# Row factor of the RMS norms: two narrow fp32 products rewritten as pairs of fp32r products over high and low halves

## The chip, the cores and the metric

The kernel runs on one core of one Trainium2 chip. The metric is the device time of one execution in microseconds. TensorE (PE in the profile, with its weight loads PEld) multiplies, VectorE (DVE), ScalarE (ACT) and GpSimd (POOL) work elementwise, and SyncE (SP) issues DMAs. Each engine runs its own instructions in a fixed order and waits on semaphores for the others.

## The reference, cut to what matters

The program is a trunk of two layers over 512 tokens of width 1024. Each layer has a SwiGLU feed-forward half step, a mixer (layer 0 a bidirectional state-space scan, layer 1 a two-dimensional neighbourhood attention), a second feed-forward half step, and a gated embedding. Every one of these starts with an RMS norm:

```python
def rmsnorm(x, g):
    xf = x.astype(jnp.float32)
    y = xf * lax.rsqrt(jnp.mean(xf * xf, axis=-1, keepdims=True) + RMS_EPS)
    return (y * g.astype(jnp.float32)).astype(x.dtype)

for i in range(DEPTH):
    h = h + 0.5 * swiglu(rmsnorm(h, ffn1_norm[i]), ffn1_w_gu[i], ffn1_w_down[i])
    hn = rmsnorm(h, mix_norm[i])
    h = h + mixer(hn)          # the state-space mixer norms its own output once more
    h = h + 0.5 * swiglu(rmsnorm(h, ffn2_norm[i]), ffn2_w_gu[i], ffn2_w_down[i])
    gate = jax.nn.sigmoid(rmsnorm(h, ple_norm[i]) @ ple_w_gate[i])
    h = h + gate * rmsnorm(p[i] @ ple_w_proj[i], ple_post_norm[i])
```

That makes eleven row factors of 512 tokens each: five per layer, and one inside the state-space mixer.

## The kernel before, in words

Activations lie transposed: 128 channels on the partitions, 512 tokens along the free dimension, eight such tiles `h[0..7]`. All large products are made of fp32r operands (fp32 rounded to fewer bits): each fp32 tensor is split into a high part, a cast to fp32r, and a low part, the rest. A product is then three matmuls, high by high, high by low and low by high, on lines 278, 281 and 282 (512 columns) or 508, 509 and 510 (256 columns, the feed-forward blocks that save a multiplication). Weights arrive by DMA as fp32 (`wr`, `md`), ACT casts the high part (L221, `wh`) and DVE subtracts the low part (L223, `wl`), up to three units ahead of TensorE.

The gain of a norm is folded into the split of `h`, and the matmuls start before the row factor is known; the factor is multiplied in when a result leaves PSUM. The factor itself is made in two steps. While the last channels of `h` are produced, ACT squares each tile (L328) and DVE or POOL adds the squares into one tile `acc` (L332). Then `begin` sums over the partitions: four fp32 matmuls, each with 128 tokens of `acc` as the stationary operand and one column of 1/1024 as the moving one (L346), which leave the means of 512 tokens as a 128x4 tile. DVE scales them (L349) and takes the reciprocal square root in two integer and nine floating operations on 128x4 elements (`newton_rsqrt`, L313 to L319, result `self.y`). Some matmuls later `end` spreads the factors again: four fp32 matmuls whose stationary operand is one column of `y`, broadcast to 128 columns, and whose moving operand is the identity (L356); ACT copies the 128x512 result to SBUF (L359), and only then can results that wait for it leave PSUM. An fp32 matmul of the program stands in the trace as two weight loads and two matmuls.

`begin` is called at eleven places. In this text they are numbered by time: 0 first feed-forward of layer 0, 1 state-space mixer, 2 the norm inside it, 3 second feed-forward, 4 norm of the embedding (`ple_proj`), 5 gate of the embedding; 6 to 10 the same for layer 1, without the inner norm: 6 feed-forward, 7 attention, 8 feed-forward, 9 embedding, 10 gate. A scheduler sets the order of each engine's instructions from the order in which they are written, their dependences and its own estimate of their lengths; at run time the order is fixed, and an instruction that waits holds up everything behind it on its engine. The tag `sq` has four buffers of 128x512.

Of the kernel before, what the change touches and what calls it, by code (L numbers as in the profile page):

```python
# [8 lines left out]
F32R = mybir.dt.float32r  # L9
I32 = mybir.dt.int32  # L10
AF = mybir.ActivationFunctionType
ALU = mybir.AluOpType
AX = mybir.AxisListType

P = 128
# [10 lines left out]
EPS = 1e-6  # L26
NH = 32
NG = 8
NC = T // P
# [41 lines left out]
def trunk(ctx, tc, A, out):  # L71
    nc = tc.nc
    v, s, g, te, sy = nc.vector, nc.scalar, nc.gpsimd, nc.tensor, nc.sync


    cp = ctx.enter_context(tc.tile_pool(name="cp", bufs=1))
# [10 lines left out]
    def nm(t):  # L87
        uid[0] += 1
        return f"{t}{uid[0]}"

    def sm(shape, dt=F32):
        return sp.tile([P] + list(shape), dt, name=nm("sm"), tag="sm", bufs=12)

    def slot(tag, bufs):
        return lambda dt=F32: bp.tile([P, T], dt, name=nm(tag), tag=tag, bufs=bufs)

    hs, t2, sc, sq = slot("hs", 8), slot("t2", 7), slot("sc", 15), slot("sq", 4)

    def md(dt=F32):
        return bp.tile([P, 2, T], dt, name=nm("md"), tag="md", bufs=24)  # L100
# [4 lines left out]
    def rt():  # L105
        return bp.tile([P, T], F32, name=nm("rt"), tag="rt", bufs=3)

    def bank(tag, bufs):
        return ps.tile([P, T], F32, name=nm("ps"), tag=tag, bufs=bufs)

    mm_bank = lambda: bank("mm", 5)
    px_bank = lambda: bank("px", 3)
# [5 lines left out]
    ones_d = cp.tile([P, P], F32, name="ones_d")  # L118
# [4 lines left out]
        te.matmul(out=idle[:, :P], lhsT=ones_d, rhs=ones_d, start=True, stop=True)  # L123
    warm = cp.tile([P, 1], F32, name="warm")
    ident = msk[:, M_ID:M_ID + P]

    def col(i):
        return cst[:, i:i + 1]
# [13 lines left out]
    stop = A.get("stage", 4 * DEPTH)  # L142
# [86 lines left out]
    def prep_next():  # L229
        item = next(todo, None)  # L230
        if item is None:
            return False
        what, a = item
        if what == "u":
            split_raw(*take())
        elif what == "g":
            group[:] = [take()[0] for _ in range(4)]
        elif what == "s":
            p, i = a
            a21, a11, a22, a12 = group  # L240
            if i == 0:
                blocks[p] = {0: a11, 2: a21, 3: wide(), 4: a12, 6: a22}
                v.tensor_add(out=blocks[p][3], in0=a21, in1=a22)
            elif i == 1:
                blocks[p][1] = blocks[p][5] = wide()
                v.tensor_sub(out=blocks[p][1], in0=blocks[p][3], in1=a11)
            else:
                v.tensor_sub(out=a21, in0=a11, in1=a21)
        else:
            p, i = a  # L250
            b = blocks[p]
            split_raw(b[i], 1024)
            if i == 1:
                v.tensor_sub(out=b[5], in0=b[4], in1=b[5])
        top_up()
        return True
# [16 lines left out]
    def gemm(pt, w, pairs, first=True, last=True, off=0, cols=slice(0, T), behind=False):  # L273
        hi, lo = w
        n = len(pairs)
        for k, xp in enumerate(pairs):
            sl = slice((off + k) * P, (off + k + 1) * P)
            m = te.matmul(out=pt, lhsT=hi[:, sl], rhs=part(xp, 0, cols), start=first and k == 0, stop=False)  # L278
            if behind and k == 0:
                tc.keep_in_program_order(m)  # L280
            te.matmul(out=pt, lhsT=hi[:, sl], rhs=part(xp, 1, cols), start=False, stop=False)  # L281
            gemm.last = te.matmul(out=pt, lhsT=lo[:, sl], rhs=part(xp, 0, cols), start=False,  # L282
                                  stop=last and k == n - 1)
# [27 lines left out]
    def newton_rsqrt(m, y, a):  # L311

        v.tensor_scalar(out=y.bitcast(I32), in0=m.bitcast(I32), scalar1=1, scalar2=None, op0=ALU.arith_shift_right)  # L313
        v.tensor_scalar(out=y.bitcast(I32), in0=y.bitcast(I32), scalar1=-1, scalar2=0x5F3759DF,
                        op0=ALU.mult, op1=ALU.add)
        for _ in range(3):
            v.tensor_mul(out=a, in0=y, in1=y)
            v.scalar_tensor_tensor(out=a, in0=a, scalar=-0.5, in1=m, op0=ALU.mult, op1=ALU.mult)
            last = v.scalar_tensor_tensor(out=y, in0=a, scalar=1.5, in1=y, op0=ALU.add, op1=ALU.mult)  # L319
        return last  # L320

    class SumSq:
# [8 lines left out]
            else:  # L331
                (v if fast else g).tensor_add(out=self.acc, in0=self.acc, in1=q)  # L332

        def rsqrt(self, scale=1.0, eps=EPS):
            pt = px_bank()
            te.matmul(out=pt, lhsT=ones_d, rhs=self.acc, start=True, stop=True)
            m, a, y = sc(), sc(), rt()
            v.tensor_scalar(out=m, in0=pt, scalar1=scale, scalar2=eps, op0=ALU.mult, op1=ALU.add)
            newton_rsqrt(m, y, a)
            return y  # L340

        def begin(self, scale=1.0, eps=EPS):

            pt = px_bank()
            for c in range(NC):
                te.matmul(out=pt[:, c:c + 1], lhsT=self.acc[:, c * P:(c + 1) * P], rhs=ones_d[:, :1],  # L346
                          start=True, stop=True)
            m, a, self.y = sm([NC]), sm([NC]), sm([NC])
            v.tensor_scalar(out=m, in0=pt[:, :NC], scalar1=scale, scalar2=eps, op0=ALU.mult, op1=ALU.add)  # L349
            self.last = newton_rsqrt(m, self.y, a)  # L350

        def end(self):

            pt = px_bank()
            for c in range(NC):
                te.matmul(out=pt[:, c * P:(c + 1) * P], lhsT=self.y[:, c:c + 1].to_broadcast([P, P]), rhs=ident,  # L356
                          start=True, stop=True)
            r = rt()
            s.copy(out=r, in_=pt)  # L359
            return r  # L360

    class Norm:
# [14 lines left out]

        def count(self, k, fast=False):
            self.ss.add(h[k], fast=fast or k == KD - 1)

        def factor(self):
            return self.ss.rsqrt()

        def begin(self, half=False):
            if half:
# [8 lines left out]
    def ffn(norm, nxt, between=None, first=None, at=4):  # L394
# [9 lines left out]
        def gate_up(f):  # L404
# [3 lines left out]
            if first and f < 2:  # L408
                held.append((f, pg, pu))
                if f == 1:  # L410
                    first([p for x in held for p in x[1:]], norm.pairs)
                    mid()
                return
# [1016 lines left out]
    def first(pts, pairs):  # L1430
        done_ = [0] * 4
        here, cut_ = 0, [0] * 4
        for o in order:
            if isinstance(o, int):
                here = o + 1
            else:
                cut_[o[0]] += 1
            for u in range(4):
                while done_[u] < min(here, 4 * cut_[u]):
                    k = done_[u]  # L1440
                    gemm(pts[u], begun[u][2:], pairs[k:k + 1], first=k == 0, last=k == KD - 1, off=k)
                    done_[u] += 1
        prep_next()

        with tc.issue_after(splits[-1].ins):
            for k in range(KD):
                n.count(k, True)
        while len(ready) < 3:
            prep_next()

    for i in range(stop):
        l, w = divmod(i, 4)
        last = i == stop - 1
        m = None if last else Norm(gains[i + 1], (lambda: md(F32R)) if w == 2 else xa)
# [112 lines left out]
```

## Time and profile before

| what | value |
|---|---|
| median of 3 runs | 2305.32 us (2305.17 to 2305.44) |
| the profiled execution's own time | 2305.77 us |
| its span, first to last instruction | 2304.0 us |
| PE busy | 2292.0 us, 99% |
| DVE busy | 1826.6 us, 79% |
| ACT busy | 1179.0 us, 51% |
| L346 (begin): loads and matmuls on PE | 88 and 88 |
| L356 (end): loads and matmuls on PE | 88 and 88 |

Times in the profile's timeline are microseconds from the start of the span: a row gives start, length, engine, line, operation, output and inputs, shape and count, and in brackets the engine's idle time before it with what ended it. Matmuls are pipelined, so the length of one (0.39 us) is longer than the step from one to the next (0.23 us); it is the steps that add up. A row of PEld is a weight load, which runs beside the matmul before it.

### The profile page before, as it was taken

To read this page: it belongs to the slowest core of one execution; us is meant where nothing else is said; L and a number is where in the kernel's file an instruction comes from. 1 tells how busy PE (TensorE), PEld (TensorE's weight loads), DVE (VectorE), ACT (ScalarE), POOL (GpSimd) and SP (SyncE) were. 2 spreads that over 40 slices of the span, in tenths; PEclk is the share of its full clock that TensorE was granted. 3 is DMA by queue.
4 is the path that set the end of the run, shared out by engine and by line. 5 is a ranking of instruction groups with operands and counts; after the bars stand their busy time and mean duration, and the time that the engine had idled before them with its cause. 6 is when DMAs were issued, how large, how long until landed. Compare 5 with 4: busy or idle time off the path is not lost.

```text
span 2304.0 us, 35426 instructions
## 1 busy us (share of the span) xinstructions
PE 2292.0 (99%) x13732; PEld 2025.5 (88%) x13732; DVE 1826.6 (79%) x2621; ACT 1179.0 (51%) x2038; POOL 323.7 (14%) x261
## 2 busy tenths in 40 slices
PE   9999999999999999999999999999999999999999
PEld 8899998888888888999998889999878888999987
DVE  7878878888788958987885897787578859887866
ACT  5433445877676864444445444444446745444452
POOL 0000001355555641000003100000110010000020
PEclk9999999999999999999999999999999999999999
DMA  5323323444444543333223233232557732333222
GB/s 185 116 83 106 110 73 130 164 155 138 146 140 151 188 158 119 106 101 106 94 78 104 101 102 107 84 102 83 165 183 220 219 119 83 111 106 101 87 92 73
DMA packets 105224, 281.69 MB, mean 122 GB/s; under 512 B 13136, under 2 KB 14032, under 8 KB 105056
## 3 DMA queue, kind: packets, MB, share of 16 engines
q1 hardware_dynamic: 104768, 279.30, 37.0%
q8 instruction: 107, 1.75, 0.3%
q14 instruction: 61, 0.50, 0.1%
q10 hardware_dynamic: 288, 0.14, 0.0%
HBM read 259.70 MB, written 13.40 MB: 119 GB/s over the span
## 4 chain that ended last, share of the span: by engine, by line
PE 95%; DVE 3%; DMA 1%; ACT 1%; issue 0%; SPq 0%; POOL 0%; ACTq 0%; POOLq 0%
PE ps L278 19%; PE ps L282 19%; PE ps L281 19%; PE ps L510 10%; PE ps L509 10%; PE ps L508 10%; PE ps L930 1%; PE ps L889 1%; PE ps L910 1%; PE ps L1325 1%; PE ps L1271 1%; DVE wl L223 1%; PE ps L845 1%; PE ps L834 1%; DVE md L304 1%; PE ps L1314 0%
## 5 line engine op out<-in xcount | busy, mean ns | idle before, releaser
L278 PE MATMUL ps<-md,wh 128*128 128x512 f32 (+1 forms) x2032 | 798.6, 393 | 0.0
L282 PE MATMUL ps<-md,wl 128*128 128x512 f32 (+1 forms) x2032 | 790.5, 389 | 1.6 <-DVE wl L223 1.6
L281 PE MATMUL ps<-md,wh 128*128 128x512 f32 (+1 forms) x2032 | 791.2, 389 | 0.0
L221 ACT CAST wh<-wr 128x1024 fp32r<-128x1024 f32 (+2 forms) x395 | 351.8, 892 | 500.9 <-PE ps L281 260.1
L223 DVE TENSOR_TENSOR wl<-wr,wh 128x1024 fp32r<-128x1024 f32 (+2 forms) x395 | 418.5, 1061 | 84.4 <-ACT wh L221 82.6
L282 PEld LDWEIGHTS ps<-md,wl 128*128 128x128 f32 x2032 | 381.5, 188 | 83.5 <-DVE wl L223 2.9
L278 PEld LDWEIGHTS ps<-md,wh 128*128 128x128 f32 x2032 | 382.2, 188 | 73.8 <-issue 0.7
L281 PEld LDWEIGHTS ps<-md,wh 128*128 128x128 f32 x2032 | 382.4, 188 | 71.5
L221 ACT CAST wh<-md 128x1024 fp32r<-128x1024 f32 x175 | 183.6, 1049 | 322.6 <-PE ps L509 296.1
L332 POOL TENSOR_TENSOR sq<-sq,sq 128x512 f32<-128x512 f32 x71 | 101.0, 1422 | 1637.7 <-ACT sq L328 1633.3
L510 PE MATMUL ps<-sc,wl 128*128 128x256 f32 x980 | 277.5, 283 | 0.8 <-DVE wl L223 0.8
L508 PE MATMUL ps<-sc,wh 128*128 128x256 f32 x980 | 276.9, 283 | 0.8 <-ACT wh L221 0.8
L509 PE MATMUL ps<-md,wh 128*128 128x256 f32 x980 | 277.4, 283 | 0.1
L510 PE MATMUL ps<-md,wl 128*128 128x256 f32 x980 | 277.3, 283 | 0.0
L509 PE MATMUL ps<-sc,wh 128*128 128x256 f32 x980 | 277.3, 283 | 0.0
L508 PE MATMUL ps<-md,wh 128*128 128x256 f32 x980 | 277.2, 283 | 0.0
L514 DVE TENSOR_TENSOR t<-ps,t 128x512 f32<-128x512 f32 x245 | 165.8, 689 | 137.6 <-PE ps L510 137.0
L223 DVE TENSOR_TENSOR wl<-md,wh 128x1024 fp32r<-128x1024 f32 x175 | 213.4, 1219 | 16.3 <-ACT wh L221 15.9
L508 PEld LDWEIGHTS ps<-sc,wh 128*128 128x128 f32 x980 | 187.7, 192 | 4.9 <-ACT wh L221 1.0
L509 PEld LDWEIGHTS ps<-sc,wh 128*128 128x128 f32 x980 | 187.7, 192 | 3.9
L509 PEld LDWEIGHTS ps<-md,wh 128*128 128x128 f32 x980 | 188.0, 192 | 1.6 <-DVE md L472 0.4
L508 PEld LDWEIGHTS ps<-md,wh 128*128 128x128 f32 x980 | 188.0, 192 | 1.3
(209 smaller groups left out, 2895.5 us busy)
## 6 DMA issues: line engine op xcount, KB each, us to landing
wr<-in_w_gw_dram SPq DMA_DIRECT2D x70, 512.0 KB, 3.5
md<-in_w_gw_dram SPq DMA_DIRECT2D x70, 512.0 KB, 5.0
wr<-in_w_in_dram SPq DMA_DIRECT2D x65, 512.0 KB, 3.5
wr<-in_w_dn_dram SPq DMA_DIRECT2D x128, 256.0 KB, 2.6
wr<-in_w_gu_dram SPq DMA_DIRECT2D x32, 512.0 KB, 3.5
hs<-crow SPq DMA_DIRECT2D x64, 256.0 KB, 3.7
wr<-in_w_dn_dram SPq DMA_DIRECT2D x32, 384.0 KB, 3.0
wr<-in_w_qkv_dram SPq DMA_DIRECT2D x24, 512.0 KB, 4.3
```

Source lines behind the costliest of these rows:

```text
L221: splits.append(s.copy(out=hi[:, :n], in_=raw[:, :n]))
L223: v.tensor_sub(out=lo[:, :n], in0=raw[:, :n], in1=hi[:, :n])
L278: m = te.matmul(out=pt, lhsT=hi[:, sl], rhs=part(xp, 0, cols), start=first and k == 0, stop=False)
L281: te.matmul(out=pt, lhsT=hi[:, sl], rhs=part(xp, 1, cols), start=False, stop=False)
L282: gemm.last = te.matmul(out=pt, lhsT=lo[:, sl], rhs=part(xp, 0, cols), start=False, stop=last and k == n - 1)
L304: split.low = v.tensor_sub(out=dst[:, 1, :], in0=src, in1=dst[:, 0, :])
L332: (v if fast else g).tensor_add(out=self.acc, in0=self.acc, in1=q)
L508: te.matmul(out=o, lhsT=hi[:, sl], rhs=xh, start=j == 0 and kk == 0, stop=False)
L509: te.matmul(out=o, lhsT=hi[:, sl], rhs=xl, start=False, stop=False)
L510: te.matmul(out=o, lhsT=lo[:, sl], rhs=xh, start=False, stop=j == 1 and kk == 3)
L514: v.tensor_add(out=k[to], in0=pt, in1=k[other])
L834: te.transpose(out=pt[:, cs(i)], in_=src[:, cs(c)], identity=ident)
```

## The change

`begin` first splits `acc`: ACT casts it to a high half in fp32r, DVE subtracts for the low half, both 128x512, in two more buffers of the tag `sq`. Its four fp32 matmuls become eight fp32r ones, two for each 128 tokens (high and low half as stationary operand, added up in PSUM), with two equal columns of 1/1024 (`mean`) as the moving operand. The mean and the reciprocal root are now 128x8 instead of 128x4. After the root, DVE splits `y` into two halves (a cast and a subtraction, 128x8). `end` becomes eight fp32r matmuls, high and low half of each column broadcast, by an fp32r copy of the identity (`identr`). `mean` and `identr` are made once, on ACT, `mean` at the very start and `identr` in the first feed-forward behind the squares. An unused function of 128x512 factors goes.

```diff
@@ -123,6 +123,9 @@
     ident = msk[:, M_ID:M_ID + P]
+    mean = cp.tile([P, 2], F32R, name="mean")
+    s.copy(out=mean, in_=ones_d[:, :2])
+    identr = cp.tile([P, P], F32R, name="identr")
@@ -331,30 +334,31 @@
         def begin(self, scale=1.0, eps=EPS):
 
+            hi, lo = sq(F32R), sq(F32R)
+            s.copy(out=hi, in_=self.acc)
+            v.tensor_sub(out=lo, in0=self.acc, in1=hi)
             pt = px_bank()
             for c in range(NC):
-                te.matmul(out=pt[:, c:c + 1], lhsT=self.acc[:, c * P:(c + 1) * P], rhs=ones_d[:, :1],
-                          start=True, stop=True)
-            m, a, self.y = sm([NC]), sm([NC]), sm([NC])
-            v.tensor_scalar(out=m, in0=pt[:, :NC], scalar1=scale, scalar2=eps, op0=ALU.mult, op1=ALU.add)
-            self.last = newton_rsqrt(m, self.y, a)
+                for x, part_ in enumerate((hi, lo)):
+                    te.matmul(out=pt[:, 2 * c:2 * c + 2], lhsT=part_[:, c * P:(c + 1) * P], rhs=mean,
+                              start=x == 0, stop=x == 1)
+            m, a, y = sm([2 * NC]), sm([2 * NC]), sm([2 * NC])
+            v.tensor_scalar(out=m, in0=pt[:, :2 * NC], scalar1=scale, scalar2=eps, op0=ALU.mult, op1=ALU.add)
+            newton_rsqrt(m, y, a)
+            self.y = sm([2, 2 * NC], F32R)
+            v.tensor_copy(out=self.y[:, 0], in_=y)
+            self.last = v.tensor_sub(out=self.y[:, 1], in0=y, in1=self.y[:, 0])
 
         def end(self):
 
             pt = px_bank()
             for c in range(NC):
-                te.matmul(out=pt[:, c * P:(c + 1) * P], lhsT=self.y[:, c:c + 1].to_broadcast([P, P]), rhs=ident,
-                          start=True, stop=True)
+                for x in range(2):
+                    te.matmul(out=pt[:, c * P:(c + 1) * P],
+                              lhsT=self.y[:, x, 2 * c:2 * c + 1].to_broadcast([P, P]), rhs=identr,
+                              start=x == 0, stop=x == 1)
             r = rt()
             s.copy(out=r, in_=pt)
             return r
@@ -1445,6 +1446,7 @@
         with tc.issue_after(splits[-1].ins):
             for k in range(KD):
                 n.count(k, True)
+        s.copy(out=identr, in_=ident)
```

Line numbers behind the change are three higher in this part of the file (L221 becomes L224, L223 L226, L328 L331, L332 L335), and the new lines are L340 (cast of `acc`), L341 (its low half), L345 (matmuls of `begin`), L348 (scale), L351 and L352 (split of `y`) and L359 (matmuls of `end`).

The change moves instructions. First place: ACT and DVE at norm 6, the first feed-forward of layer 1. ACT before:

```order
L306 ACTIVATE md_12767<-hs_8795,cst 128x512
L328 ACTIVATE sq_12770<-hs_8795 128x512
L221 CAST wh_12791<-wr_12693 128x1024
L221 CAST wh_12876<-wr_12795 128x1024
L359 COPY rt_12899<-ps_12894 128x512
```

ACT now:

```order
L309 ACTIVATE md_12861<-hs_8844,cst 128x512
L331 ACTIVATE sq_12864<-hs_8844 128x512
L340 CAST sq_12939<-sq_12596 128x512
L224 CAST wh_12885<-wr_12787 128x1024
L224 CAST wh_12981<-wr_12889 128x1024
L363 COPY rt_13008<-ps_12999 128x512
```

The cast of `acc` stands ahead of two weight casts. DVE at the end of the same norm's root, before (L319 is the last operation of the root, L243 the first of the next feed-forward's weight sums):

```order
L317 TENSOR_TENSOR sm_12851<-sm_12852 128x4
L318 SCALAR_TENSOR_TENSOR sm_12851<-sm_12851,sm_12850 128x4
L319 SCALAR_TENSOR_TENSOR sm_12852<-sm_12851,sm_12852 128x4
L243 TENSOR_TENSOR md_12869<-wr_12779,md_12787 128x1024
L246 TENSOR_TENSOR md_12871<-md_12869,wr_12785 128x1024
```

DVE now:

```order
L320 TENSOR_TENSOR sm_12953<-sm_12954 128x8
L321 SCALAR_TENSOR_TENSOR sm_12953<-sm_12953,sm_12952 128x8
L322 SCALAR_TENSOR_TENSOR sm_12954<-sm_12953,sm_12954 128x8
L351 CAST sm_12967<-sm_12954 128x8
L352 TENSOR_TENSOR sm_12967<-sm_12954,sm_12967 128x8
L246 TENSOR_TENSOR md_12974<-wr_12873,md_12881 128x1024
```

Two operations more stand between the root and everything behind it on DVE. Second place: ACT in the first feed-forward of the program, behind norm 0, where casts of activations (L441 and L303 are a SiLU and a split, L471 and L492 splits of sums) stand among casts of weights (L221). Before:

```order
L441 ACTIVATE t_463<-t_463 128x512
L471 CAST sc_411<-t_472 128x256
L303 CAST md_469<-t_466 128x512
L221 CAST wh_527<-wr_350 128x1024
L303 CAST md_478<-t_474 128x512
L492 CAST sc_481<-t_485 128x512
```

Now:

```order
L442 ACTIVATE t_482<-t_482 128x512
L224 CAST wh_546<-wr_365 128x1024
L306 CAST md_488<-t_485 128x512
L472 CAST sc_430<-t_491 128x256
L306 CAST md_497<-t_493 128x512
L493 CAST sc_500<-t_504 128x512
```

The weight cast has moved ahead of the two casts L303 and L471. Third place: PE at norm 4, the embedding's, whose `begin` stands among the products of a feed-forward's last chunk. Before, it stood between two groups of eighteen matmuls:

```order
L281 MATMUL ps_12185<-md_11960,wh_12123 128x512
L282 MATMUL ps_12185<-md_11959,wl_12125 128x512
L346 MATMUL ps_12217<-ones_d,sq_12034 128x1 x4
L278 MATMUL ps_12237<-md_11367,wh_12154 128x512
L281 MATMUL ps_12237<-md_11368,wh_12154 128x512
```

Now:

```order
L285 MATMUL ps_12312<-md_11731,wl_12220 128x512
L345 MATMUL ps_12285<-mean,sq_12281 128x2
L281 MATMUL ps_12312<-md_12023,wh_12218 128x512
L284 MATMUL ps_12312<-md_12024,wh_12218 128x512
L285 MATMUL ps_12312<-md_12023,wl_12220 128x512
L345 MATMUL ps_12285<-mean,sq_12282 128x2
L345 MATMUL ps_12285<-mean,sq_12281 128x2
```

It has moved twelve matmuls later, and its first matmul, on the high half, stands three matmuls ahead of the second, on the low half. Norm 9 moves in the same way. At the other nine norms `begin` stands at the same place on PE, and `end` at the same place or, at norms 1, 6 and 7, one matmul later.

More of the change, by code (lines that the diff above doesn't have):

```diff
@@ L332, in add @@
                 (v if fast else g).tensor_add(out=self.acc, in0=self.acc, in1=q)
[L334 to L340, printed above, removed]
         def begin(self, scale=1.0, eps=EPS):
+            hi, lo = sq(F32R), sq(F32R)
+            s.copy(out=hi, in_=self.acc)
+            v.tensor_sub(out=lo, in0=self.acc, in1=hi)
             pt = px_bank()
             for c in range(NC):
-                te.matmul(out=pt[:, c:c + 1], lhsT=self.acc[:, c * P:(c + 1) * P], rhs=ones_d[:, :1],
-                          start=True, stop=True)
-            m, a, self.y = sm([NC]), sm([NC]), sm([NC])
-            v.tensor_scalar(out=m, in0=pt[:, :NC], scalar1=scale, scalar2=eps, op0=ALU.mult, op1=ALU.add)
-            self.last = newton_rsqrt(m, self.y, a)
+                for x, part_ in enumerate((hi, lo)):
[7 more added lines that the diff above has]
+            self.last = v.tensor_sub(out=self.y[:, 1], in0=y, in1=self.y[:, 0])
         def end(self):
@@ L379, in count @@
             self.ss.add(h[k], fast=fast or k == KD - 1)
-        def factor(self):
-            return self.ss.rsqrt()
         def begin(self, half=False):
```

## The prediction

> **What bounds the kernel now.** I read the page first, then the chain of waits, then the timeline at each of the eleven norms.
>
> ```profile
> span 2304.0 us, 35426 instructions
> PE 2292.0 (99%) x13732; PEld 2025.5 (88%) x13732; DVE 1826.6 (79%) x2621; ACT 1179.0 (51%) x2038; POOL 323.7 (14%) x261
> ...
> PE 95%; DVE 3%; DMA 1%; ACT 1%; issue 0%; SPq 0%; POOL 0%; ACTq 0%; POOLq 0%
> ```
>
> PE is busy for 99% of the span and holds 95% of the chain that ended last: what makes PE's own stream shorter is gained in full, and what makes PE wait is lost in full. So there are two questions: what do the narrow products take of PE, and how much time is there between `acc` and `begin`, and between `y` and `end`? The timeline at norm 10 answers the first:
>
> ```profile
> 2256.51 0.68 DVE L332 TENSOR_TENSOR sq<-sq,sq 128x512 f32<-128x512 f32 x1
> 2258.14 0.39 PE L282 MATMUL ps<-md,wl 128*128 128x512 f32 x1
> 2258.82 0.39 PE L282 MATMUL ps<-md,wl 128*128 128x512 f32 x1
> 2258.82 1.08 PEld L346 LDWEIGHTS ps<-ones_d,sq 128*128 128x128 f32 x8
> 2259.82 0.19 PEld L278 LDWEIGHTS ps<-md,wh 128*128 128x128 f32 x1
> 2259.94 0.19 PEld L281 LDWEIGHTS ps<-md,wh 128*128 128x128 f32 x1
> 2260.18 0.40 PE L281 MATMUL ps<-md,wh 128*128 128x512 f32 x1
> ...
> 2265.21 0.39 PE L282 MATMUL ps<-md,wl 128*128 128x512 f32 x1
> 2265.21 1.08 PEld L356 LDWEIGHTS ps<-msk,sm 128*128 128x128 f32 x8
> 2266.56 0.39 PE L281 MATMUL ps<-md,wh 128*128 128x512 f32 x1
> ```
>
> Three matmuls of 512 columns take 2258.82 - 2258.14 = 0.68, so one step is 0.227. From the L282 ahead of `begin` to the L281 behind it are two such steps, 0.45, but 2260.18 - 2258.82 = 1.36 pass: `begin` takes 0.91 of PE. `end` takes 2266.56 - 2265.21 - 0.45 = 0.90. Both hold eight weight loads, and both come to eight times 0.113, although one has matmuls of 1 column and the other of 128: **the loads set the pace, not the matmuls**. The fp32r loads behind them, L278 and L281, also stand 0.12 apart.
>
> **The change on PE: about nothing.** Four fp32 products were eight loads and eight matmuls; eight fp32r products are eight loads and eight matmuls. Is an fp32r load shorter? The groups of instructions, one row for fp32r and one for fp32, with busy time and mean ns:
>
> ```profile
> L281 PEld LDWEIGHTS ps<-md,wh 128*128 128x128 f32 x2032 | 382.4, 188 | 71.5
> L356 PEld LDWEIGHTS ps<-msk,sm 128*128 128x128 f32 x88 | 11.2, 189 | 2.1 <-DVE sm L319 1.1 <-issue 0.5
> ```
>
> 188 against 189 ns: no. The narrowest fp32r products that the trace has are these, of 256 columns:
>
> ```profile
> 1347.34 0.28 PE L508 MATMUL ps<-md,wh 128*128 128x256 f32 x1
> ...
> 1347.46 0.28 PE L509 MATMUL ps<-md,wh 128*128 128x256 f32 x1
> ```
>
> Their step is 0.12. With 0.227 for 512 columns, 256 columns cost 0.107 and each product 0.013 beside; 128 columns would be 0.067 and 2 columns 0.014, both below a load. So I price each of the 176 pieces at 0.113 as before: 0. The upper bound is the 256-column step, 0.120: +1.2 us. The lower bound is a piece that only its matmul sets: 0.067, or 176 x 0.046 = -8.1 us; the two load rows speak against it, and I take the value by them.
>
> The Trainium skill speaks for the change here: "FP8 and Floating Point Precision", TensorE Precision Notes, counts four passes for a true fp32 product, and one stands for reduced precision; by passes alone eleven `end`s would halve from eight pieces of two passes. The trace disagrees on what is saved, since eight pieces take 0.90 with two passes of 128 columns and 0.91 with two passes of one.
>
> **Waits at begin: +2.1 us.** Before, PE could load as soon as `acc` was added up. Now ACT casts 128x512 and DVE subtracts 128x512 in between. The nearest groups, same shape and types:
>
> ```profile
> L492 ACT CAST sc<-t 128x512 fp32r<-128x512 f32 x24 | 14.9, 619 | 9.6 <-DVE t L490 5.4 <-DVE t L489 4.1
> L493 DVE TENSOR_TENSOR sc<-t,sc 128x512 fp32r<-128x512 f32 x24 | 16.4, 683 | 0.0
> ```
>
> 0.62 + 0.68 and three hand-overs of 0.05 (from L319 to the load of `end`, below) make 1.45 from `acc` to the first low half, which PE wants one load (0.11) after the high one. So a norm stalls for 1.34 less its slack. Norm 10 has 2258.82 - 2257.19 = 1.63: none, and norm 5 is alike. These three have less:
>
> ```profile
> 361.31 0.68 DVE L332 TENSOR_TENSOR sq<-sq,sq 128x512 f32<-128x512 f32 x1
> 362.18 0.26 ACT L659 ACTIVATE ea<-ea 128x64 f32<-128x64 f32 x1
> 362.70 0.19 PEld L346 LDWEIGHTS ps<-ones_d,sq 128*128 128x128 f32 x1
> ...
> 898.55 0.68 DVE L332 TENSOR_TENSOR sq<-sq,sq 128x512 f32<-128x512 f32 x1
> 900.28 0.19 PEld L346 LDWEIGHTS ps<-ones_d,sq 128*128 128x128 f32 x1
> ...
> 1307.76 0.68 DVE L332 TENSOR_TENSOR sq<-sq,sq 128x512 f32<-128x512 f32 x1
> 1309.04 0.41 PEld L346 LDWEIGHTS ps<-ones_d,sq 128*128 128x128 f32 x2
> ```
>
> Norm 3: slack 900.28 - 899.23 = 1.05, stall 0.29. Norm 6: 1309.04 - 1308.44 = 0.60, stall 0.74. Norm 1: 0.71, and the cast stands behind the exponential L659 that ends at 362.44, so its low half is ready at 362.44 + 0.62 + 0.68 + 0.10 = 363.84 and wanted at 362.81: 1.03. Sum 2.06. The other norms have slack of 2 us and more, or (4 and 9) `begin` moved later. What is queued behind the new cast on ACT is a weight cast, wanted by PE several microseconds later.
>
> **The longer root: +0.9 us at end.** Two operations more of 128x8 stand between the root and `end`. The operations of the root follow each other every 0.20 (L318 to L319 below), so `y` is 0.40 later.
>
> ```profile
> 32.36 0.16 DVE L319 SCALAR_TENSOR_TENSOR sm<-sm,sm 128x4 f32<-128x4 f32 x1
> 32.65 1.08 PEld L356 LDWEIGHTS ps<-msk,sm 128*128 128x128 f32 x8
> ...
> 857.77 0.41 PEld L356 LDWEIGHTS ps<-msk,sm 128*128 128x128 f32 x3 [0.37 <-DVE sm L319]
> ...
> 1314.25 0.16 DVE L318 SCALAR_TENSOR_TENSOR sm<-sm,sm 128x4 f32<-128x4 f32 x1
> 1314.45 0.16 DVE L319 SCALAR_TENSOR_TENSOR sm<-sm,sm 128x4 f32<-128x4 f32 x1
> 1314.53 1.23 DVE L243 TENSOR_TENSOR md<-wr,md 128x1024 f32<-128x1024 f32 x1
> 1314.73 0.63 PEld L356 LDWEIGHTS ps<-msk,sm 128*128 128x128 f32 x5 [0.47 <-issue]
> ```
>
> Norm 0: `y` at 32.52, load at 32.65; the low half is ready at 32.97 and wanted at 32.76: +0.21. Norm 2 already waits for L319 (in brackets), and on DVE its root is mixed with weight subtractions that come later too: +0.5 (0.3 to 0.8). Norms 1, 6 and 7 wait now as well, but there `end` has moved a matmul (0.23) later: 0.40 - 0.11 - 0.23, 0.06 each, 0.2 in all.
>
> **DVE-bound stretches: +1.7 us.** Three stages end up waiting for DVE, which was full from the root on:
>
> ```profile
> 51.08 1.05 ACT L221 CAST wh<-wr 128x1024 fp32r<-128x1024 f32 x1 [1.01 <-DMA wr<-in_w_gu_dram]
> 54.90 0.50 PE L282 MATMUL ps<-md,wl 128*128 128x512 f32 x1 [0.99 <-DVE wl L223]
> ...
> 1330.00:1340.00 10.00, 10.00 (x45) 8.24 (x45) 9.98 (x18) 4.98 (x8) 0.00 (x0) 1.00 0.18 52
> ...
> 1349.03 0.39 PE L510 MATMUL ps<-sc,wl 128*128 128x256 f32 x1 [0.81 <-DVE wl L223]
> ...
> 944.05 0.68 DVE L223 TENSOR_TENSOR wl<-wr,wh 128x512 fp32r<-128x512 f32 x1
> ```
>
> (The third row is the table by windows: PE, PEld, DVE 9.98 of 10 us busy.) After norm 6, DVE is late by 0.74 + 0.40 and PE waits for it at 1349, so PE ends 1.14 late, 0.34 more than at `end`. After norm 1, a matmul more ahead of `end` makes the factor 0.23 later for a stage of the same kind. In the first feed-forward two casts now stand behind a weight cast that waits for its DMA at 51.08 (the front part's second place): DVE's L304s come after it, its L223 at about 54.4 instead of 53.62, PE 0.8 late, 0.6 more than at `end`. In the second feed-forwards (norms 3 and 8) L223 ends at 944.73, and PE's matmul on it starts at 944.88, 0.15 later; DVE runs without a gap from the root to there, so 0.40 - 0.15 = 0.25 each, 0.5 in all.
>
> **Norms 4 and 9: +0.5 us.** `begin` moved 12 x 0.227 later and has three matmuls inside it.
>
> ```profile
> 1236.38 0.16 DVE L319 SCALAR_TENSOR_TENSOR sm<-sm,sm 128x4 f32<-128x4 f32 x1
> 1239.60 0.41 PEld L356 LDWEIGHTS ps<-msk,sm 128*128 128x128 f32 x2
> ```
>
> The slack at `end` was 1239.60 - 1236.54 = 3.06; 2.72 + 0.68 + 0.40 is 0.74 more than that. Part of the root stood behind other DVE work, which now overlaps; between 0 and 0.74 I take 0.25 each.
>
> At the start, `mean` costs ACT a table load and a cast, and `identr` a cast of 0.3; both lie where ACT waits for DMAs (its idle time): 0, or 0.3 if that cover is gone.
>
> **Sum.** 0 + 2.1 + 0.9 + 1.7 + 0.5 = +5.2 us on a span of 2304.0, 2309.2; the profiled execution took 2305.77, so 2311.0, and the median of the runs is 0.45 below it: **2310.5 us**, +0.22%.
>
> **Rivals.** *The lateness is absorbed.* The orders moved behind each norm, and wherever a weight subtraction got ahead of elementwise work the terms of the DVE-bound stretches and of norms 4 and 9 vanish. What is left is 2.1 + 0.9 = 3.0: 2308.3. For it: the waits after `y` were reckoned with the old times; against: DVE had no idle time there to absorb with. *Narrow fp32r pieces are faster (the other side).* If the matmul sets the pace, the lower bound of -8.1 applies from 0.113 down to 0.067; it outweighs the waits from 5.2 / 176 = 0.030 saved per piece on. -8.1 + 5.2 = -2.9: 2302.4. For it: no fp32r load stands in the trace with a narrow matmul of its own kind on either side; against: 188 against 189 ns. The Trainium skill has a rule of this kind: "TensorE: Matmul & The Clock Gate", Weight-path perf modes, turns a faster weight load on for 128 weights of a type that is not fp32, and names no gain for 4-byte data; the trace's 188 ns say that fp32r does not get it. *Narrow fp32r products are slower.* All fp32r rows have 256 columns or more. If 128 columns took four passes of 0.053, 0.213 a piece, each `end` would grow by 8 x 0.10 = 0.8: +8.8, 2319.3. Nothing in the trace excludes it, and no row shows it.
>
> **How the numbers follow.** Forecast 0.47, with its own range 2307.5 to 2313 (norm 2, norms 4 and 9, the first feed-forward and +1.2 for the pieces); absorbed 0.30; faster pieces 0.10; slower pieces 0.13. Two in ten outside: 2303.5 to 2315. This kernel's runs tell apart about 0.2%, 4.6 us: the line to slower is 2309.9. It cuts the forecast near its middle (0.6 above), the absorbed case seldom (0.1), the slower pieces lie above it whole: 0.28 + 0.03 + 0.13 = 0.44, which I round to 0.46 for waits that I did not see. Faster (below 2300.7) is half the faster pieces and a little of the absorbed: 0.08. Same: 0.46.
>
> **What would show it.** Right: `begin` and `end` still 0.91 and 0.90 of PE where nothing waits; loads of L345 waiting for DVE L341 at norms 1, 3 and 6; L359 waiting for L352 at norms 0, 1, 2, 6 and 7; the waits near 54 and 1349 longer. Wrong: a step between pieces clearly off 0.113 either way, or waits at `begin` of norms that I gave slack.

## The result and the profile after

The changed kernel takes 2315.03 us (median of 4 runs, 2314.72 to 2317.24), the kernel before 2305.24 us (4 runs). The ratio is 1.0044, with a 95% interval of 1.0032 to 1.0056: slower, by 9.8 us. The prediction said 2310.5 us, with a range up to 2315.0. So the sign was right, the size was half of what came, and the time lies just past the upper end of the range. The profiled execution took 2314.72 us.

The head of the page, and its chain of waits by engine:

```profile
span 2312.9 us, 35475 instructions
PE 2295.7 (99%) x13732; PEld 2025.7 (88%) x13732; DVE 1837.4 (79%) x2654; ACT 1186.1 (51%) x2052; POOL 323.8 (14%) x261
...
PE 88%; DVE 9%; ACT 1%; issue 1%; DMA 0%; POOL 0%; ACTq 0%; POOLq 0%; SPq 0%; DVEq 0%
```

PE has as many matmuls and loads as before. DVE has 10.8 us more to do and now holds 9% of the chain that ended last, where it held 3%: the time was lost where PE waits for DVE.

**The pieces.** The timeline at norm 10, where nothing waits; the rows answer to those at 2258.14 and 2265.21 in the prediction:

```profile
2267.77 0.39 PE L285 MATMUL ps<-md,wl 128*128 128x512 f32 x1
2267.77 1.08 PEld L345 LDWEIGHTS ps<-mean,sq 128*128 128x128 f32 x8
2267.99 0.95 PE L345 MATMUL ps<-mean,sq 128*128 128x2 f32 x8
2268.80 0.49 PE L281 MATMUL ps<-md,wh 128*128 128x512 f32 x1
...
2274.16 0.39 PE L285 MATMUL ps<-md,wl 128*128 128x512 f32 x1
2274.16 1.08 PEld L359 LDWEIGHTS ps<-identr,sm 128*128 128x128 f32 x8
2275.51 0.39 PE L284 MATMUL ps<-md,wh 128*128 128x512 f32 x1
```

Eight loads start within the same 1.08 us as before. From the L285 ahead of `begin` to the L281 behind it 1.03 pass; before, at norm 9, 2232.13 - 2231.10 = 1.03 (rows below). For `end`, from 2274.16 to the second matmul behind it, 1.35; before, 2266.56 - 2265.21 = 1.35. The fp32r pieces cost what the fp32 pieces cost.

**Where the 8.9 us of the spans went.** With the pieces of `begin` and `end` left out, the k-th matmul of the one trace is nearly everywhere the k-th of the other. The start in the new trace less the start in the old one is PE's lateness there, and each of its steps is a loss at one place:

| place | predicted | measured |
|---|---|---|
| start of the program | 0 | -0.23 |
| norm 0, `end` | 0.21 | 0.14 |
| first feed-forward, wait near 54.9 | 0.6 | 0.62 |
| norm 1, `begin` | 1.03 | 0.76 |
| norm 1, `end`, and the stage behind it | 0.06 + 0.23 | 0.12 + 0.20 |
| norm 2, `end` | 0.5 | 0.29 |
| norm 3, `begin` | 0.29 | 0.10 |
| second feed-forwards | 0.25 + 0.25 | 0.41 + 0.40 |
| **norms 4 and 9** | **0.25 + 0.25** | **2.04 + 2.04** |
| ahead of norm 6 | 0 | 0.44 |
| norm 6, `begin` | 0.74 | 0.70 |
| norm 6, `end`, and the stage behind it | 0.06 + 0.34 | 0.44 + 0.40 |
| norm 7, `end` | 0.06 | 0.10 |
| sum | 5.1 | 9.0 |

The prediction's own sum, 5.2, is that of its rounded terms. The last matmul starts 8.92 later than before; the few hundredths to 9.0 are small steps that the table leaves out.

The start differs from one execution to the next (in the nine traces of this kernel and of those below, the first products came 0.1 to 1.0 us earlier than in the trace of before, with and without the change's two constants), so a few tenths of the single trace belong to no change. The medians lie 9.8 apart, the two profiled executions 8.95; the table can place the latter only.

**Norms 4 and 9** hold 4.1 of the 8.9. The timeline of the changed kernel at norm 9, all engines:

```profile
2222.65 7.48 POOL L335 TENSOR_TENSOR sq<-sq,sq 128x512 f32<-128x512 f32 x5 [0.57 <-ACT sq L331]
...
2240.30 0.61 ACT L340 CAST sq<-sq 128x512 fp32r<-128x512 f32 x1
2240.54 1.29 POOL L335 TENSOR_TENSOR sq<-sq,sq 128x512 f32<-128x512 f32 x1 [2.78 <-ACT sq L331]
2240.96 0.19 PEld L345 LDWEIGHTS ps<-mean,sq 128*128 128x128 f32 x1 [0.27 <-ACT sq L340]
2240.96 0.27 PE L345 MATMUL ps<-mean,sq 128*128 128x2 f32 x1
2241.87 0.69 DVE L341 TENSOR_TENSOR sq<-sq,sq 128x512 fp32r<-128x512 f32 x1 [1.17 <-POOL sq L335]
2242.62 0.94 PE L345 MATMUL ps<-mean,sq 128*128 128x2 f32 x7 [0.58 <-DVE sq L341]
2243.59 0.17 DVE L348 TENSOR_SCALAR sm<-ps 128x8 f32<-128x8 f32 x1 [1.03 <-PE ps L345]
...
2248.08 0.39 PE L285 MATMUL ps<-md,wl 128*128 128x512 f32 x1
2248.98 0.17 DVE L351 CAST sm<-sm 128x8 fp32r<-128x8 f32 x1
2249.18 0.17 DVE L352 TENSOR_TENSOR sm<-sm,sm 128x8 fp32r<-128x8 f32 x1
2249.20 1.20 PE L359 MATMUL ps<-identr,sm 128*128 128x128 f32 x8 [0.73 <-DVE sm L351]
```

And of the kernel before, at the same norm:

```profile
2231.10 0.39 PE L282 MATMUL ps<-md,wl 128*128 128x512 f32 x1
2231.10 1.08 PEld L346 LDWEIGHTS ps<-ones_d,sq 128*128 128x128 f32 x8
2232.13 0.49 PE L278 MATMUL ps<-md,wh 128*128 128x512 f32 x1
2232.31 0.16 DVE L349 TENSOR_SCALAR sm<-ps 128x4 f32<-128x4 f32 x1
...
2237.00 0.16 DVE L319 SCALAR_TENSOR_TENSOR sm<-sm,sm 128x4 f32<-128x4 f32 x1
2240.21 1.08 PEld L356 LDWEIGHTS ps<-msk,sm 128*128 128x128 f32 x8
```

Norm 9's `acc` was complete at 2222.65 + 7.48 = 2230.13, yet its cast runs at 2240.30. The subtraction then waits 1.17 us for POOL's L335, which adds a square for *another* norm (10, the gate's). That is not a wait for data. The order of instructions, with the numbers of the tiles, shows what is shared (POOL's additions, ACT's square and cast, DVE's subtraction):

```
L335 TENSOR_TENSOR sq_22278<-sq_22278,sq_22363 128x512
L335 TENSOR_TENSOR sq_22395<-sq_22395,sq_22426 128x512
L335 TENSOR_TENSOR sq_22395<-sq_22395,sq_22458 128x512
...
L331 ACTIVATE sq_22458<-hs_18859 128x512
L340 CAST sq_22461<-sq_22278 128x512
...
L341 TENSOR_TENSOR sq_22462<-sq_22278,sq_22461 128x512
```

At that moment the four `sq` buffers hold norm 9's sum (22278), norm 10's sum (22395), a square on its way into it (22458), and the new high half (22461). The low half (22462) gets the square's buffer (the program gives 22458 and 22462 the same address), and that comes free when POOL has added the square, at 2240.54 + 1.29 = 2241.83. The shared buffers would also explain the order that stood in the text before the prediction: `begin` twelve matmuls later, with its low half three matmuls behind the high one. The first experiment tests that. `begin` lost 0.93 (the loads' waits for L340 and L341, and the torn group), and `end` 1.11, since `y` was complete at 2249.35 and PE was there at 2248.31.

**The other waits** are of the kinds predicted. PE at `begin` of norms 1 and 6, PE just ahead of norm 6, and DVE and PE in the second feed-forward of layer 0:

```profile
363.51 0.69 DVE L341 TENSOR_TENSOR sq<-sq,sq 128x512 fp32r<-128x512 f32 x1 [1.00 <-ACT sq L340]
364.26 0.86 PEld L345 LDWEIGHTS ps<-mean,sq 128*128 128x128 f32 x7 [0.54 <-DVE sq L341]
364.26 0.94 PE L345 MATMUL ps<-mean,sq 128*128 128x2 f32 x7 [0.46 <-DVE sq L341]
...
1312.10 0.75 DVE L310 SCALAR_TENSOR_TENSOR md<-hs,cst,md 128x512 fp32r<-128x512 f32 x1 [0.79 <-ACT md L309]
1312.91 0.50 PE L284 MATMUL ps<-md,wh 128*128 128x512 f32 x1 [0.18 <-DVE md L310]
1314.14 0.69 DVE L341 TENSOR_TENSOR sq<-sq,sq 128x512 fp32r<-128x512 f32 x1 [0.69 <-ACT sq L340]
1314.89 0.86 PEld L345 LDWEIGHTS ps<-mean,sq 128*128 128x128 f32 x7 [0.54 <-DVE sq L341]
...
946.34 0.67 DVE L226 TENSOR_TENSOR wl<-wr,wh 128x512 fp32r<-128x512 f32 x1
947.07 0.50 PE L285 MATMUL ps<-md,wl 128*128 128x512 f32 x1 [0.18 <-DVE wl L226]
```

Two steps at norm 6 need a closer look. Its `end` lost 0.44, far more than at norm 1 or 7, and the stage behind it lost its time at 1340.03 and not at the later wait for DVE that the prediction had named (the last row):

```profile
1315.87 0.17 DVE L348 TENSOR_SCALAR sm<-ps 128x8 f32<-128x8 f32 x1 [1.03 <-PE ps L345]
1316.30 1.23 DVE L226 TENSOR_TENSOR wl<-wr,wh 128x1024 fp32r<-128x1024 f32 x1 [0.27 <-ACT wh L224]
...
1340.03 0.50 PE L285 MATMUL ps<-md,wl 128*128 128x512 f32 x1 [0.17 <-DVE wl L226]
...
1355.45 0.38 PE L511 MATMUL ps<-sc,wl 128*128 128x256 f32 x1 [0.81 <-DVE wl L226]
```

The root of norm 6 held a stall of 0.27 on DVE. The cast that the profile names for it had ended at 1316.00, so what DVE waited for stays open. In the trace of the first experiment below, with the same order of instructions there, L226 follows L348 at once (1313.57 behind 1313.48), and that `end` lost 0.08. So most of the 0.44 does not follow from the order of instructions; whether other executions of the changed kernel have the stall, no run shows. The last row is the wait that stood at 1349.03 before: 0.81 then and 0.81 now.

### The profile page after: what moved, and what is told of

It reads as the page before. It is cut to its first block, busy times and chain, and to the rows that moved or that the text cites. A ratio compares the mean times of both kernels' runs of the same rounds, so it can differ in the third digit from the quotient of the medians.

```text
span 2312.9 us, 35475 instructions
## 1 busy us (share of the span) xinstructions
PE 2295.7 (99%) x13732; PEld 2025.7 (88%) x13732; DVE 1837.4 (79%) x2654; ACT 1186.1 (51%) x2052; POOL 323.8 (14%) x261
## 4 chain that ended last, share of the span: by engine, by line
PE 88%; DVE 9%; ACT 1%; issue 1%; DMA 0%; POOL 0%; ACTq 0%; POOLq 0%; SPq 0%; DVEq 0%
PE ps L281 17%; PE ps L285 17%; PE ps L284 17%; PE ps L511 10%; PE ps L510 10%; PE ps L509 10%; DVE wl L226 2%; DVE md L307 1%; PE ps L931 1%; PE ps L890 1%; PE ps L1272 1%; PE ps L911 1%; PE ps L1326 1%; PE ps L846 1%; PE ps L835 1%
## 5 line engine op out<-in xcount | busy, mean ns | idle before, releaser
L281 PE MATMUL ps<-md,wh 128*128 128x512 f32 (+1 forms) x2032 | 798.3, 393 | 0.0
L285 PE MATMUL ps<-md,wl 128*128 128x512 f32 (+1 forms) x2032 | 791.0, 389 | 2.9 <-DVE wl L226 2.9
L224 ACT CAST wh<-wr 128x1024 fp32r<-128x1024 f32 (+2 forms) x395 | 351.7, 892 | 480.6 <-PE ps L284 285.2
L226 DVE TENSOR_TENSOR wl<-wr,wh 128x1024 fp32r<-128x1024 f32 (+2 forms) x395 | 418.2, 1060 | 82.6 <-ACT wh L224 80.2
L285 PEld LDWEIGHTS ps<-md,wl 128*128 128x128 f32 x2032 | 381.5, 188 | 85.5 <-DVE wl L226 5.3
L281 PEld LDWEIGHTS ps<-md,wh 128*128 128x128 f32 x2032 | 382.3, 188 | 73.7 <-issue 0.7
L224 ACT CAST wh<-md 128x1024 fp32r<-128x1024 f32 x175 | 183.5, 1049 | 320.4 <-PE ps L510 298.6
L335 POOL TENSOR_TENSOR sq<-sq,sq 128x512 f32<-128x512 f32 x71 | 101.0, 1423 | 1645.7 <-ACT sq L331 1004.1
L226 DVE TENSOR_TENSOR wl<-md,wh 128x1024 fp32r<-128x1024 f32 x175 | 213.4, 1220 | 16.8 <-ACT wh L224 16.6
```

The lines of the kernel that those rows point to most:

```text
L224: splits.append(s.copy(out=hi[:, :n], in_=raw[:, :n]))
L226: v.tensor_sub(out=lo[:, :n], in0=raw[:, :n], in1=hi[:, :n])
```

## The experiments

Where a text below says "late", it is PE's lateness against the kernel before, taken as in the table.

### Spare buffers for the halves at norms 4 and 9

```diff
-        def begin(self, scale=1.0, eps=EPS):
-            hi, lo = sq(F32R), sq(F32R)
+        def begin(self, scale=1.0, eps=EPS, alloc=sq):
+            hi, lo = alloc(F32R), alloc(F32R)
...
-        yield pp, (lambda: ss.begin(4.0, 4.0 * EPS)), finish
+        yield pp, (lambda: ss.begin(4.0, 4.0 * EPS, t2)), finish
```

> The changed kernel, with the two halves of `acc` at norms 4 and 9 taken from the tag `t2` and not from `sq`; nothing else. Theory (too few `sq` buffers): at these two norms the subtraction L341 waited for GpSimd's L335 to give back a fourth `sq` buffer, and the scheduler had put `begin` twelve matmuls later for that. With spare buffers `begin` stands where it stood before the change; TensorE then waits for cast and subtraction, 1.34 less the 0.24 us that lay between `acc` and `begin`, 1.10 us a norm, and nothing at `end`, which has 3 us. The two norms cost 1.10 each and not 2.04: 2315.0 - 1.9 = 2313.1 us. Rival (the split and the longer root cost this wherever they stand): 2 us each as before, 2315.0 us.

Measured: 2310.95 us (9 runs, 2309.91 to 2311.38), ratio to before 1.0024 (1.0014 to 1.0034). That is 4.1 us less than the change, all that the two norms had cost. Most other steps stayed (0.78 and 0.11 at norm 1, 0.42 and 0.38 in the second feed-forwards, 1.13 ahead of norm 6 and at its `begin`). Two did not: `end` of norm 6 lost 0.08 in place of 0.44, and `begin` of norm 0 lost 0.25 in place of nothing. The timeline at norm 9:

```profile
2227.42 0.62 ACT L340 CAST t<-sq 128x512 fp32r<-128x512 f32 x1 [2.09 <-POOL sq L335]
2228.08 0.69 DVE L341 TENSOR_TENSOR t<-sq,t 128x512 fp32r<-128x512 f32 x1 [1.84 <-ACT t L340]
...
2235.26 1.08 PEld L345 LDWEIGHTS ps<-mean,t 128*128 128x128 f32 x8
2244.38 1.08 PEld L359 LDWEIGHTS ps<-identr,sm 128*128 128x128 f32 x8
```

With two buffers more, the cast follows the last addition at once, `begin` stands where it stood before the change, and PE waits at neither place. The theory of the buffers holds, and the rival falls. The expectation still asked for 1.10 of waiting a norm: it had taken POOL's addition for norm 10 (0.24 us ahead of `begin`) for the end of norm 9's `acc`. The halves are ready at 2228.77, 6.5 us before they are wanted.

### `begin` alone, and `end` alone

In the first the root and `end` are as before (with 128x8 in the root), in the second `acc`, the four products on it and the mean are as before, and the split of `y` and the eight pieces of `end` stay.

```diff
-            newton_rsqrt(m, y, a)
-            self.y = sm([2, 2 * NC], F32R)
-            v.tensor_copy(out=self.y[:, 0], in_=y)
-            self.last = v.tensor_sub(out=self.y[:, 1], in0=y, in1=self.y[:, 0])
+            self.last = newton_rsqrt(m, self.y, a)
...
-                              lhsT=self.y[:, x, 2 * c:2 * c + 1].to_broadcast([P, P]), rhs=identr,
+                          lhsT=self.y[:, 2 * c:2 * c + 1].to_broadcast([P, P]), rhs=ident,
```

> The change in `begin` alone: `acc` split, eight fp32r products; the root without a split, `end` with four fp32 products as before. Theory (the changed kernel's lateness is the sum of waits at single norms, and pieces cost nothing): the waits at begin of norms 1, 3 and 6 (0.76, 0.10, 1.14) stay, and norms 4 and 9 lose only the 0.40 of the two operations: 0.93 + 0.70 each. 0.76 + 0.10 + 1.14 + 3.26 = 5.3 over 2305.2: 2310.5 us. Rival (the fp32r products themselves are slower or faster than the fp32 ones): TensorE's steps in `begin` off 0.112, and a time away from 2310.5 by eight times that for each of eleven norms.

```diff
-            hi, lo = sq(F32R), sq(F32R)
-            s.copy(out=hi, in_=self.acc)
-            v.tensor_sub(out=lo, in0=self.acc, in1=hi)
...
-                for x, part_ in enumerate((hi, lo)):
-                    te.matmul(out=pt[:, 2 * c:2 * c + 2], lhsT=part_[:, c * P:(c + 1) * P], rhs=mean,
+                te.matmul(out=pt[:, c:c + 1], lhsT=self.acc[:, c * P:(c + 1) * P], rhs=ones_d[:, :1],
```

> The change in `end` alone: `begin` with four fp32 products on `acc` as before, root on 128x4, then the split of `y` and eight fp32r products. Theory (sum of waits): norms 4 and 9 have 3 us at `end` and cost nothing, nothing waits at `begin`; what is left is the two operations, 0.40 us, at the ends that were tight (norms 0, 1, 2 and 6, 0.1 to 0.4 each) and in the DVE-bound stretches behind norms 0, 1, 3, 6 and 8 (0.2 to 0.6 each): 2.0 to 3.2 over 2305.2, 2307.2 to 2308.4 us. Rival (the costs of norms 4 and 9 come from the longer root): 1 us more for each of them, 2309.2 us and above.

Measured: `begin` alone 2311.23 us (8 runs; 1.0025, 1.0015 to 1.0036), `end` alone 2309.42 us (11 runs; 1.0019, 1.0010 to 1.0028). The two losses, 5.8 and 4.0, add up to the change's 9.8, as a sum of separate waits should. Place by place they add up less well: norms 4 and 9 lost 3.6 in the one and nothing in the other, where the change lost 4.1, and norm 2 lost 0.22 and 0.55, where the change lost 0.29.

In `begin` alone, norms 4 and 9 are late by 0.97 + 0.82 and 0.96 + 0.82 (expected 0.93 + 0.70), norm 1 by 0.78. In front of norm 6 nothing is lost, so the 0.44 there is the longer root's. Norm 0 lost 0.89 at `begin` (its order differs: another weight subtraction stands ahead of the last squares), of which 0.56 came back at the wait near 54.9.

In `end` alone, norms 4 and 9 cost nothing, against the rival, whose time (2309.2 and above) it would fit: the places decide. The total is 1 us above the upper end of what was expected: the root is 0.40 us longer, and 0.44 to 0.58 is lost at each of five places (norm 2, both second feed-forwards, ahead of norm 6 and in the stage behind it). The trace's steps add up to 3.5 us without the start; the other 0.5 of the runs' 4.0 is not placed. (In its profiled execution, which took 2311.35 us, 1.06 went to one wait for a DMA in the attention that no other trace has.)

### Two more operations behind the root

```diff
             v.tensor_copy(out=self.y[:, 0], in_=y)
+            for _ in range(2):
+                v.tensor_sub(out=self.y[:, 1], in0=y, in1=self.y[:, 0])
             self.last = v.tensor_sub(out=self.y[:, 1], in0=y, in1=self.y[:, 0])
```

> The change in `end` alone, with the subtraction for the low half of `y` made three times: two more DVE operations of 128x8 behind the root, 0.40 us. Theory (DVE has no idle time between the root and several later waits, so that each 0.20 added there is paid at each of them): 0.40 more at the waits of both second feed-forwards, ahead of norm 6 and in the stage behind it, 1.6, and 0.4 to 0.8 at the ends of norms 0, 1, 2 and 6, where `end` has moved one or two matmuls later: 2309.4 + 2.0 to 2.4 = 2311.4 to 2311.8 us. Rival (the lateness there comes from where the scheduler put the instructions, not from DVE's work): 2309.4 us within 0.5.

Measured: 2311.25 us (9 runs, 2310.95 to 2312.2), 1.8 above `end` alone: just under what the theory gave, and far from the rival. But the places are not all those named. The second feed-forwards are late by 0.75 and 0.79 (0.49 and 0.53 with `end` alone) and the stage behind norm 6 by 0.71 (0.58); 0.43 and 0.41 came at the `end` of norms 4 and 9, which had had 3 us of room: there the added operations were mixed with larger DVE work, so that the split's last operation ended at 2245.74, 3.64 us after the root's last at 2242.10. Ahead of norm 6, where the theory named 0.40 more, 0.44 was lost and with `end` alone 0.46; at the wait near 54.9 the loss even fell, from 0.57 to 0.35. So added work on DVE costs time by itself, but not at each later wait: eleven roots with two operations of 0.20 are 4.4 us of DVE time, which cost 4.0 us the first time (`end` alone) and 1.8 the second.

### The two constants alone

```diff
     ident = msk[:, M_ID:M_ID + P]
+    mean = cp.tile([P, 2], F32R, name="mean")
+    s.copy(out=mean, in_=ones_d[:, :2])
+    identr = cp.tile([P, P], F32R, name="identr")
...
                 n.count(k, True)
+        s.copy(out=identr, in_=ident)
```

> The kernel before with the two constants of the change alone: `mean` at the start and `identr` behind the squares of the first feed-forward, both written and never read. Theory (both lie where ACT waits for DMAs): 2305.3 us, and the wait near 54.9 us as long as before. Rival (the extra cast moves the order of the first feed-forward, and that is what cost 0.62 there): 2305.9 us.

Measured: 2305.67 us (11 runs; 1.0001, 0.9992 to 1.0010), and no loss near 54.9. The constants are hidden. What moved the first feed-forward is the `end` part of the change, since `end` alone is 0.57 late there and `begin` alone is not. The wait itself, in the changed kernel:

```profile
52.98 0.39 PE L284 MATMUL ps<-md,wh 128*128 128x512 f32 x1
54.97 0.50 PE L285 MATMUL ps<-md,wl 128*128 128x512 f32 x1 [1.61 <-DVE wl L226]
```

Before, PE went on from there at 54.90, after a wait of 0.99 (in the prediction's rows). The weight's low half comes at the same time in both, 0.07 apart. PE had done two matmuls less ahead of it (before, two more started at 53.29 and 53.52), and reached the wait 0.09 earlier: 0.45 + 0.09 + 0.07 = 0.61.

### A rounded sum: half the pieces of `begin`

```diff
-                (v if fast else g).tensor_add(out=self.acc, in0=self.acc, in1=q)
+                to = self.acc if self.left else sq(F32R)
+                (v if fast else g).tensor_add(out=to, in0=self.acc, in1=q)
+                self.acc = to
...
-                te.matmul(out=pt[:, c:c + 1], lhsT=self.acc[:, c * P:(c + 1) * P], rhs=ones_d[:, :1],
+                te.matmul(out=pt[:, 2 * c:2 * c + 2], lhsT=self.acc[:, c * P:(c + 1) * P], rhs=mean,
```

(`left` counts the squares that are still to come.)

> The kernel before, with one thing else: the last addition of squares writes its sum rounded to fp32r, into a buffer of its own, and `begin` makes four fp32r products of it (two equal columns) in place of four fp32 ones; the low half of `acc` is left out. No cast, no subtraction, no split of `y`. Theory (the loads set the pace): four pieces fewer a norm at 0.112, 0.45 us for each of eleven norms: 2305.2 - 4.9 = 2300.3 us. Rival (TensorE comes earlier to stretches where DVE or a weight is late, and the gain is given back there): half of it, 2302.8 us. If the products and not the loads set the pace, four fp32 products of one column save nothing like that, and `begin` goes down by less or more than half.

Measured: 2301.48 us (11 runs, 2300.11 to 2302.83), ratio to before 0.9984 (0.9975 to 0.9993): faster than both kernels, by 3.9 and 13.6 us. Every one of the eleven norms brought 0.41 to 0.46, and 1.3 was given back: 0.30 at the `end` of norm 2, which waits for `y`, and 0.99 in the stage behind norm 6:

```profile
1330.14 1.22 DVE L225 TENSOR_TENSOR wl<-wr,wh 128x1024 fp32r<-128x1024 f32 x1
1331.41 0.50 PE L284 MATMUL ps<-md,wl 128*128 128x512 f32 x1 [0.66 <-DVE wl L225]
```

Theory and rival both had a share: the pieces cost what the loads cost, and about a quarter of the gain (1.3 of 4.9) stopped at places where PE waits for DVE.

### Each rounded piece twice

```diff
+                for x in range(2):
-                te.matmul(out=pt[:, 2 * c:2 * c + 2], lhsT=self.acc[:, c * P:(c + 1) * P], rhs=mean,
-                          start=True, stop=True)
+                    te.matmul(out=pt[:, 2 * c:2 * c + 2], lhsT=self.acc[:, c * P:(c + 1) * P], rhs=mean,
+                              start=x == 0, stop=x == 1)
```

> The kernel with the rounded sum, with each of the four fp32r products of `begin` made twice and added up (the factor 0.5 stands in the scale): eight fp32r pieces where the kernel before has eight fp32 ones, and no cast, subtraction or split beside. Theory (fp32 and fp32r pieces cost the same): the time of the kernel before, 2305.3 us, with a step of 0.112. Rival (fp32r pieces are dearer or cheaper): 88 times the difference of the steps.

Measured: 2306.03 us (11 runs; 1.0003, 0.9994 to 1.0012): no difference that can be told. At norm 10 eight fp32r pieces, with no split beside them:

```profile
2259.24 0.39 PE L284 MATMUL ps<-md,wl 128*128 128x512 f32 x1
2259.25 1.08 PEld L354 LDWEIGHTS ps<-mean,sq 128*128 128x128 f32 x8
2260.60 0.40 PE L283 MATMUL ps<-md,wh 128*128 128x512 f32 x1
```

2260.60 - 2259.24 = 1.36, the span of eight fp32 pieces in the prediction's rows. This trace ends 0.4 us later; one step at the `end` of norm 2, 0.49, is more than all of it.

### A rounded factor as well: half the pieces of `end`

```diff
-            self.last = newton_rsqrt(m, self.y, a)
+            self.y = sm([2 * NC], F32R)
+            self.last = newton_rsqrt(m, y, a, self.y)
...
-                te.matmul(out=pt[:, c * P:(c + 1) * P], lhsT=self.y[:, 2 * c:2 * c + 1].to_broadcast([P, P]), rhs=ident,
+                te.matmul(out=pt[:, c * P:(c + 1) * P], lhsT=self.y[:, 2 * c:2 * c + 1].to_broadcast([P, P]), rhs=identr,
```

> The kernel of the run before with the rounded sum (four fp32r products in `begin`), and now `end` in the same way: the last operation of the root writes `y` rounded to fp32r, and `end` makes four fp32r products of it; the low half of `y` is left out as well. Theory (a piece costs one load, 0.112): 44 pieces fewer again, 4.9 us, of which up to 0.45 each is given back where a stage ends up waiting for DVE (first feed-forward, both second feed-forwards, and the stage behind norm 6, where the run before gave back 0.99): 2296.6 to 2298.4 us. Rival (a piece of 128 columns is set by its own stream and not by its load): the step inside `end` differs from 0.112, and the gain from 0.45 a norm.

Measured: 2297.52 us (5 runs, 2297.09 to 2298.82), ratio to before 0.9965 (0.9953 to 0.9978), 8.0 us faster than before and 17.5 faster than the change. Four loads in place of eight at norm 10:

```profile
2257.41 0.39 PE L285 MATMUL ps<-md,wl 128*128 128x512 f32 x1
2257.41 0.64 PEld L365 LDWEIGHTS ps<-identr,sm 128*128 128x128 f32 x4
2258.31 0.39 PE L284 MATMUL ps<-md,wh 128*128 128x512 f32 x1
```

2258.31 - 2257.41 = 0.90 in place of 1.35: the same 0.45 for four pieces of 128 columns as for four of two columns. Of the 22 halved groups all but one bring 0.39 to 0.48, 9.4 in all (at `begin` of norm 6 most of the gain is lost again at the wait just ahead of it, and 0.07 is left); 1.7 is given back at the four places expected (0.23 near 54.9, 0.46 in each second feed-forward, 0.57 behind norm 6).

## Why the prediction was right and where it was wrong

- **"The change on PE: about nothing."** Right. 0.113 a piece was measured as 0.11 in `begin` and `end`, with two columns and with 128, and eight fp32r pieces alone in place of eight fp32 ones made no difference. With that, both rivals on the price of a piece fall, the faster ones (2302.4) and the slower ones (2319.3). The Trainium skill, in "FP8 and Floating Point Precision", TensorE Precision Notes, counts four passes for a true fp32 product. That count does not show in the pace of these products: `end` took 1.35 with its two neighbours before and after the change. What halved its own share was leaving out four pieces, each with its load.
- **"Waits at begin: +2.1 us."** The mechanism and the norms were right: L345 waits for L341 at norms 1, 3 and 6, measured 0.76, 0.10 and 0.70, 1.6 in all. Cast and subtraction took 0.62 and 0.69, as taken. Norms 1 and 3 lost 0.2 to 0.3 less than reckoned. A likely reason, not tested: a load normally starts ahead of its matmul (0.22 at norm 10, 2267.77 and 2267.99), and at norm 1 load and matmul start together at 364.26, so that the lead covered a part of the wait. At norm 6, which lost 0.70 of 0.74, load and matmul start together too, so the lead can't be the whole of it.
- **"Norms 4 and 9: +0.5 us."** This is the step that failed: 4.1 us. The prediction read the move of `begin` by twelve matmuls as a move with nothing but its length, set 2.72 + 0.68 + 0.40 against 3.06 of room, got 0.74, and then took a third of it. It did not ask why the scheduler had moved it, and counted the later place as slack for `begin`. `sq` has four buffers, and at these two norms two sums are alive at once, with a square on its way; the two halves want a fifth buffer. So `begin` waited as well (0.93 a norm, not counted at all), and the root did not get shorter by overlap but longer: from L348 at 2243.59 to the end of L352 at 2249.35 it took 5.76, against 2237.16 - 2232.31 = 4.85 before. 2.72 + 0.68 + 0.91 exceed the room by 1.3; 1.11 was measured. With spare buffers the whole term is gone. The Trainium skill names such a sign in "Perfetto Trace Analysis", Optimization Strategy: the same gap repeating for a stretch of the kernel, on the engine that should be saturated, can mean that there isn't enough memory for the next tile. Here the gap does not fill a stretch, it comes at two places; the cause agrees: PE waits 0.58 us for a subtraction that waits 1.17 us for an addition which has nothing to do with its data.
- **"The longer root" and "DVE-bound stretches": +2.6 us.** 3.1 us in all, of which about 0.36 is the stall at norm 6 that another trace does not have; without it that `end` lost 0.08 for 0.06. The first feed-forward (0.62 for 0.6) had the size by luck: the weight cast that was to hold up two others started at 49.88 and not at 51.08, L226 ended at the same time as before, and PE had less work ahead of it. Behind norm 6 the loss came at 1340.03 and not at the wait of 1349. The second feed-forwards cost 0.40 each and not 0.25: PE's matmul started 0.06 behind L226 (947.01 and 947.07), but one matmul of 256 columns that had stood ahead of it now stands behind it. One place was not seen, 0.44 ahead of norm 6; `end` alone has it too (0.46) and `begin` alone has not, so it comes with the longer root. Norm 2 was taken at 0.5 and cost 0.29.
- **"The lateness is absorbed" (2308.3)** fell: the stretches did not give the time back. That waits for DVE do absorb is seen from the other side, where the rounded kernels came early and lost 1.3 and 1.7 us at them.
- **The sum** without norms 4 and 9 was 4.7, and 4.9 was measured (5.1 without the start). What carried the time out of the range is one term, 4.1 us where 0.5 was taken. That the other terms came so near in sum is in part luck: 0.44 ahead of norm 6 was not foreseen and the stall at norm 6 has no term, while norms 1, 2 and 3 cost less than reckoned.

Open: which rule of the scheduler put two matmuls less ahead of the wait near 54.9. The runs show only that it comes with the split of `y`. Open too is what DVE waited for at norm 6.

## What to carry to other kernels

Price narrow matmuls by their weight loads: here, turning one fp32 product into two fp32r ones changed nothing that could be told, and leaving a half out saved its piece, 0.11 us. Before new temporaries go into a shared set of buffers, count what is alive at every call, not at the typical one; and where a comparison of orders shows a group moved and torn, look for the buffer it waits for before pricing the move. Short operations on an engine that others wait for are not hidden: two of 0.20 us behind each of eleven roots, 4.4 us of DVE time, cost 4.0 us in `end` alone, while two more cost 1.8. So look at each place for the wait that they lengthen.

## What the runs showed of the hardware

An fp32 piece of one column, an fp32r piece of two and pieces of 128 columns of either kind follow each other about every 0.11 us within a group: eight of them take 0.90 to 0.91 us (2260.18 - 2258.82 less 0.45 in fp32, 2260.60 - 2259.24 less 0.45 in fp32r), four take 0.45. An fp32r load and an fp32 load of 128x128 both last about 0.19 us.
